# Two more weight sums moved from adding DMA transfers to VectorE, in ten units of a decoder layer

## The chip, the cores and the metric

The kernel runs on one core of a Trainium2 chip. The metric is the device time of one execution in microseconds (us), lower is better. TensorE (PE) multiplies, VectorE (DVE) and ScalarE (ACT) work elementwise, GpSimd (POOL) issues the adding DMA transfers, SyncE (SP) issues the plain loads in the order of its own queue. All five run their own instruction lists in order and meet only at semaphores.

## The reference

One layer on x of 512 positions by 2048 channels, all float32. The part that matters is a set of large products with weights:

```python
h = rmsnorm(x, norm_g[l])
proj = h @ w_in[l]                    # 2048 x 13312, three mixers and their gates
(a_u, a_b, a_c, a_z, b_v, b_g, b_z, c_u, c_z, gates) = jnp.split(proj, SPLIT_POINTS, axis=-1)
y_a = short_conv_mixer(...)           # 3-tap conv, then @ w_br_a (1024 x 2048)
y_b = conformer_conv_mixer(...)       # 31-tap conv, layernorm, then @ w_br_b
y_c = pool_mixer(...)                 # causal means, group products, then @ w_br_c
g = jax.nn.sigmoid(gates.reshape(bsz, seq, N_BRANCH, D_MODEL))
merged = g[:, :, 0] * y_a + g[:, :, 1] * y_b + g[:, :, 2] * y_c
x = x + merged @ w_o[l]               # 2048 x 2048
return rmsnorm(x, final_g)
```

## The kernel before

**Units, products, stages.** Every product with `w_in` and `w_o` is cut into units of 1024 output columns (`UNITS`: two of `glu`, four of `prod`/`side`, two of `pool`, one `zed`, six `gate`; then two for `w_o`). In a unit, positions and inner channels are halved, and a Strassen scheme makes seven products instead of eight. Each product needs one combination of the unit's four weight quarters 11, 12, 21, 22, and each combination is handled in four blocks of 128 x 1024 values (512 KB). One block of one product is a stage, so a unit has 28 stages, numbered through the program: the fourth gate unit is stages 336 to 363, the third is 308 to 335, the first unit of `w_o` is 468 to 495. Tiles carry the number: `wl350` belongs to stage 350.

**A stage.** The raw block is split into a high part (`wh`, a rounding cast by ACT, line 171) and a low part (`wl = raw - wh`, a subtraction by DVE, line 172), and TensorE makes twelve multiplications of 512 columns: lines 443 and 444 read `wh`, line 445 reads `wl`. `wh` and `wl` have three buffers each, so ACT and DVE work up to three stages ahead of TensorE.

**Where the combinations come from.** `PRODUCTS` lists the seven in order. "load" is a plain load issued by SP into a new raw tile (line 141). "add" is a transfer issued by POOL that adds a second block from memory into the raw tile already there (line 143), which can start only when the split of the block before has read that tile. "sum" is an addition by DVE of another raw tile that is loaded anyway (line 151). Raw tiles of tag A have four buffers for a unit's `11`, `s1`, `s2`, `22`; those of tag B have a ring of six for `s4`, `s3`, `12`.

```python
PRODUCTS = (
    ("11", "A", "load", 0, 0),
    ("s1", "A", "add", 0, 1),
    ("s2", "A", "sum", 1, 1),
    ("s4", "B", "load", 1, 1),
    ("s3", "B", "add", 0, 1),
    ("12", "B", "load", 1, 0),
    ("22", "A", "add", 1, 0),
)
```

**What sets the order.** `plan()` gives each transfer the stage before which it stands in the program, and a list scheduler then orders every engine's instructions; splits and sums go ahead of other DVE work where both could run. DVE work that is not about weights (31-tap convolution, line 584; centring; pooling; the activation of branch B, lines 655 to 661; joins of partial products, line 456) is handed out at a fixed rate per half stage while the units run. Its inputs (`c`, `z`, `cu`, `cz`, line 230) are loaded through the same SP queue as the raw tiles, and so are the residual rows `y` (line 1002) during `w_o`.

Of the kernel before, what the change touches and what calls it, by code (L numbers as in the profile page):

```python
# [8 lines left out]
F32 = mybir.dt.float32  # L9
# [4 lines left out]
P = 128  # L14
# [14 lines left out]
RAW = 2 * CH  # L29
# [16 lines left out]
UNITS = [("glu", B_V + c, B_G + c) for c in (0, CH)]  # L46
for _c in (0, CH):
# [10 lines left out]
# [6 lines that stand above are left out]
    ("12", "B", "load", 1, 0),  # L64
    ("22", "A", "add", 1, 0),
)
EARLY = (PRODUCTS[0], PRODUCTS[5], *PRODUCTS[1:5], PRODUCTS[6])
FIRST = (PRODUCTS[0], PRODUCTS[5], PRODUCTS[1], ("s2", "A", "add", 1, 1), *PRODUCTS[3:5], PRODUCTS[6])
STEPS = KD // 4


def block(unit, row, col, s):
    return ((unit * 2 + row) * 2 + col) * STEPS + s
# [4 lines left out]
WO_UNIT = WO_AT // (4 * STEPS)  # L78
# [8 lines left out]
def stages():  # L87

    out = []

    def seven(u, products):
        for name, tag, what, row, col in products:
            key = (u, tag, name == "12")
            out.extend((tag, key + (s,), what, block(u, row, col, s)) for s in range(STEPS))

    for u in range(len(UNITS)):
        seven(u, PRODUCTS if u else FIRST)
    for n, b in enumerate(range(BR_AT, WO_AT)):
        out.append(("AB"[n % 2], b, "load", b))
    for u in range(2):  # L100
        seven(WO_UNIT + u, EARLY if u else PRODUCTS)
    return out


class Weights:
# [3 lines left out]
    def __init__(self, tc, nc, pools, parts, src, load_ahead, split_ahead):  # L109
        self.tc, self.nc, self.pools, self.parts, self.src = tc, nc, pools, parts, src  # L110
        self.load_ahead, self.split_ahead = load_ahead, split_ahead
        self.stages = stages()
        self.last = {s[1]: n for n, s in enumerate(self.stages)}
        self.raw, self.held, self.done = {}, {}, {}
        self.events = deque(self.plan())
        self.summed = self.split = self.at = 0

    def plan(self):


        need, before, out = {}, {}, []
        for n, (_, key, what, b) in enumerate(self.stages):
            if what == "sum":
                need[b] = n - 2
            else:
                need.setdefault(b, n)
        for n, (_, key, what, b) in enumerate(self.stages):
            if what == "load":
                out.append((min(need[b], n) - self.load_ahead, n))
            elif what == "add":  # L130
                out.append((max(n - self.load_ahead, before[key] + 1), n))
            before[key] = n
        return sorted(out)

    def transfer(self):
        n = self.events.popleft()[1]
        tag, key, what, b = self.stages[n]
        if what == "load":
            t = self.raw[key] = self.held[b] = self.pools[tag].tile([P, RAW], F32, tag=tag, name=f"raw{tag}{n}")
            for at in self.pieces(n):  # L140
                self.nc.sync.dma_start(out=t[:, at], in_=self.src[b][:, at])
        else:
            self.nc.gpsimd.dma_start(out=self.raw[key], in_=self.src[b], accum_op=ALU.add)  # L143

    def sum_to(self, n):
        while self.summed < min(n, len(self.stages)):
            _, key, what, b = self.stages[self.summed]
            if what == "sum":
                t = self.raw[key]
                with self.tc.high_priority(AHEAD):  # L150
                    self.nc.vector.tensor_tensor(out=t, in0=t, in1=self.held[b], op=ALU.add)
            self.summed += 1
# [959 lines left out]
```

## Time and profile before

| quantity | value |
|---|---|
| median of 3 runs | 1652.32 us (1649.66 to 1655.26) |
| the profiled execution | 1651.81 us, of which 1650.1 us are the span |
| PE, DVE, ACT busy, share of the span | 98%, 72%, 48% |
| adding transfers of POOL (A and B) | 140 + 68, 512 KB each |
| plain raw loads of SP (A and B) | 91 + 160, 512 KB each |

The span is the time from the first to the last instruction that the profiler saw; the rest of the execution's time lies around it. Busy shares are averages over the whole span, and an engine that is busy 98% leaves little room, so what counts is where TensorE waits. A line such as `[2.67 <-DVE wl L172]` behind an instruction says that its engine sat idle for 2.67 us before it and that the end of a DVE instruction of line 172 ended that wait.

### The profile page before, as it was taken

The page shows a single profiled execution, that of the slowest core. Times are in us where ns is not written, and L with a number is a line of the kernel's source. Part 1 is how long each engine was busy: PE and PEld are TensorE (multiplying, and loading weights), DVE is VectorE, ACT ScalarE, POOL GpSimd, SP SyncE. Part 2 cuts the span into 40 slices and gives each one's busy share as a digit, 9 for nine tenths or more (in the row PEclk, how much of TensorE's full clock was granted, in tenths as well). Part 3 has the DMA queues.
Part 4 walks back from the last instruction along what each step waited for, and adds up shares of the span by engine and source line. Part 5 has one row for each costly group of instructions (what it writes and reads, how often), then busy time and mean ns, then how long its engine had stood idle before and what let it go on. Part 6 is the DMA issues. An engine that isn't in the chain of part 4 may idle for free.

```text
span 1650.1 us, 19665 instructions
## 1 busy us (share of the span) xinstructions
PE 1617.2 (98%) x7212; PEld 1330.2 (81%) x7212; DVE 1191.3 (72%) x1459; ACT 786.4 (48%) x1011; POOL 181.0 (11%) x215
## 2 busy tenths in 40 slices
PE   7899999999999999999999999999999999999997
PEld 5788887788888888888888878888888888888786
DVE  4866699899979969977778876555743444477766
ACT  6755443444444454456645454444731311345544
POOL 1201011111102020201010101010100000002010
PEclk9999999999999999999999999999999999999999
DMA  9978685968777797789989898878994633357865
GB/s 306 239 198 200 171 192 117 225 148 206 149 202 148 200 209 192 166 232 241 297 186 281 207 294 170 232 171 257 236 316 144 196 102 90 116 142 165 218 152 151
DMA packets 113744, 324.43 MB, mean 197 GB/s; under 512 B 12528, under 2 KB 16752, under 8 KB 113648
## 3 DMA queue, kind: packets, MB, share of 16 engines
q0 software_dynamic: 29952, 109.07, 36.0%
q1 hardware_dynamic: 64544, 179.50, 34.1%
q10 hardware_dynamic: 19152, 34.62, 5.7%
q8 instruction: 56, 0.92, 0.2%
q14 instruction: 40, 0.33, 0.1%
HBM read 287.48 MB, written 35.65 MB: 196 GB/s over the span
## 4 chain that ended last, share of the span: by engine, by line
PE 72%; issue 16%; DMA 6%; DVE 2%; POOL 2%; ACT 1%; SPq 0%; POOLq 0%; ACTq 0%; DVEq 0%
PE X L445 11%; PE X L443 11%; PE X L444 11%; PE Z L445 5%; PE Z L443 5%; PE Z L444 5%; PE y L897 4%; PE y L898 4%; PE y L899 4%; DMA rawB<-wts 3%; PE V L443 3%; PE V L444 3%; PE V L445 3%; POOL rawA L143 2%; DMA rawA<-wts 2%
## 5 line engine op out<-in xcount | busy, mean ns | idle before, releaser
L172 DVE TENSOR_TENSOR wl<-rawA,wh 128x1024 fp32r<-128x1024 f32 (+1 forms) x297 | 360.8, 1217 | 191.7 <-ACT wh L171 185.6
L171 ACT CAST wh<-rawA 128x1024 fp32r<-128x1024 f32 (+1 forms) x297 | 311.6, 1051 | 390.5 <-PE X L444 117.4
L172 DVE TENSOR_TENSOR wl<-rawB,wh 128x1024 fp32r<-128x1024 f32 x228 | 277.9, 1221 | 206.8 <-ACT wh L171 205.2
L171 ACT CAST wh<-rawB 128x1024 fp32r<-128x1024 f32 x228 | 238.9, 1052 | 328.6 <-PE y L898 93.2
L143 POOL DMA_DIRECT2D rawA<-wts x140 | 121.1, 865 | 1299.8 <-DVE wl L172 1262.2
L443 PE MATMUL X<-wh,xs 128*128 128x512 f32 x544 | 213.7, 393 | 3.9 <-ACT wh L171 3.8
L444 PE MATMUL X<-wh,xs 128*128 128x512 f32 x544 | 213.2, 392 | 0.0
L443 PE MATMUL Z<-wh,xs 128*128 128x512 f32 x544 | 211.4, 390 | 1.7 <-ACT xs L362 1.1
L444 PE MATMUL Z<-wh,xs 128*128 128x512 f32 x544 | 212.0, 390 | 0.7 <-DVE xs L363 0.7
L443 PE MATMUL X<-wh,x 128*128 128x512 f32 x528 | 207.2, 394 | 4.2 <-ACT x L362 4.0
L444 PE MATMUL X<-wh,x 128*128 128x512 f32 x528 | 206.8, 392 | 1.1 <-DVE x L363 1.1
L445 PE MATMUL X<-wl,xs 128*128 128x512 f32 x544 | 192.7, 393 | 7.2 <-DVE wl L172 7.0
L445 PE MATMUL Z<-wl,xs 128*128 128x512 f32 x544 | 192.5, 390 | 0.2
L445 PE MATMUL X<-wl,x 128*128 128x512 f32 x528 | 190.9, 395 | 0.0
L584 DVE SCALAR_TENSOR_TENSOR conv<-v,prm,conv 128x511 f32<-128x511 f32 (+14 forms) x240 | 168.5, 727 | 0.0
L897 PE MATMUL y<-wh,u 128*128 128x512 f32 x384 | 149.7, 390 | 0.0
L899 PE MATMUL y<-wl,u 128*128 128x512 f32 x384 | 149.7, 390 | 0.0
L898 PE MATMUL y<-wh,u 128*128 128x512 f32 x384 | 149.7, 390 | 0.0
L445 PEld LDWEIGHTS X<-wl,xs 128*128 128x128 f32 x544 | 102.1, 189 | 31.7 <-DVE wl L172 10.9
L443 PEld LDWEIGHTS X<-wh,xs 128*128 128x128 f32 x544 | 103.0, 189 | 28.1 <-ACT wh L171 6.6
L443 PEld LDWEIGHTS Z<-wh,xs 128*128 128x128 f32 x544 | 102.0, 188 | 24.2 <-ACT xs L362 1.5
L443 PEld LDWEIGHTS X<-wh,x 128*128 128x128 f32 x528 | 99.5, 189 | 26.0 <-ACT x L362 4.5
(174 smaller groups left out, 2102.6 us busy)
## 6 DMA issues: line engine op xcount, KB each, us to landing
rawB<-wts SPq DMA_DIRECT2D x160, 512.0 KB, 4.6
rawA<-wts POOLq DMA_DIRECT2D x140, 512.0 KB, 6.9
rawA<-wts SPq DMA_DIRECT2D x91, 512.0 KB, 4.2
rawB<-wts POOLq DMA_DIRECT2D x68, 512.0 KB, 8.8
g<-g SPq DMA_DIRECT2D x48, 256.0 KB, 5.0
d<-turn ACTq DMA_DIRECT2D x32, 256.0 KB, 6.4
g<-snap ACTq DMA_DIRECT2D x24, 256.0 KB, 5.4
g<-gate ACTq DMA_DIRECT2D x24, 256.0 KB, 5.7
```

The costliest lines, as they stand in the source:

```text
L143: self.nc.gpsimd.dma_start(out=self.raw[key], in_=self.src[b], accum_op=ALU.add)
L171: self.nc.scalar.copy(out=h[:, at], in_=raw[:, at])
L172: self.nc.vector.tensor_tensor(out=l[:, at], in0=raw[:, at], in1=h[:, at].bitcast(F32), op=ALU.subtract)
L443: T.matmul(p, lhsT=xh, rhs=h, start=start and k == 0, stop=False, skip_group_check=True)
L444: T.matmul(p, lhsT=xl, rhs=h, start=False, stop=False, skip_group_check=True)
L445: T.matmul(p, lhsT=xh, rhs=l, start=False, stop=k == KB - 1, skip_group_check=True)
L584: V.scalar_tensor_tensor(out=c[:, s:], in0=v[:, : S - s], scalar=pcol(P_BW, i * CONV_B + CONV_B - 1 - s), in1=c[:, s:], op0=ALU.mult, op1= ...
L897: T.matmul(banks[t], lhsT=uh[:, tk], rhs=h, start=k == 0, stop=False)
L898: T.matmul(banks[t], lhsT=ul[:, tk], rhs=h, start=False, stop=False)
L899: T.matmul(banks[t], lhsT=uh[:, tk], rhs=l, start=False, stop=k == KB - 1)
```

## The change

In the units of `pool`, `zed` and `gate` and in the first unit of `w_o` (ten units), two of the three "add" products become DVE sums (`ROOM`). For `s3` a new kind, "both", loads its block into a raw tile of its own and DVE then adds the raw tile of `s4` to it. For `22`, DVE adds the raw tile of `12`, which is loaded anyway, so no transfer is left. The last unit of `w_o` gets only the `s3` part (`EARLY`). `s1` stays an adding transfer.

```diff
+ROOM = (*PRODUCTS[:4], ("s3", "B", "both", 0, 1), PRODUCTS[5], ("22", "A", "sum", 1, 0))
+EARLY = (PRODUCTS[0], PRODUCTS[5], *PRODUCTS[1:4], ROOM[4], PRODUCTS[6])
...
-        seven(u, PRODUCTS if u else FIRST)
+        seven(u, ROOM if UNITS[u][0] in ("pool", "zed", "gate") else PRODUCTS if u else FIRST)
...
-        seven(WO_UNIT + u, EARLY if u else PRODUCTS)
+        seven(WO_UNIT + u, EARLY if u else ROOM)
...
             if what == "sum":
-                need[b] = n - 2
+                need[b] = min(need.get(b, n), n - 2)
...
+            elif what == "both":
+                out.append((n - 2 - self.load_ahead, n))
...
-        if what == "load":
-            t = self.raw[key] = self.held[b] = self.pools[tag].tile([P, RAW], F32, tag=tag, name=f"raw{tag}{n}")
+        if what in ("load", "both"):
+            t = self.raw[key] = self.pools[tag].tile([P, RAW], F32, tag=tag, name=f"raw{tag}{n}")
...
+            if what == "load":
+                self.held[b] = t
...
-            if what == "sum":
+            if what in ("sum", "both"):
                 t = self.raw[key]
+                if what == "both":
+                    b += 2 * STEPS
                 with self.tc.high_priority(AHEAD):
                     self.nc.vector.tensor_tensor(out=t, in0=t, in1=self.held[b], op=ALU.add)
```

Over the program POOL loses 84 adding transfers (44 of `s3`, 40 of `22`), SP gains 44 plain loads, and DVE gains 84 sums. In the changed kernel the sum stands on line 160, the split's subtraction on line 181, the plain load on line 146, the join on line 465, the fill on line 239 and the residual load on line 1011.

DVE in the fourth gate unit, before, from the split of the first `s4` block on (`rawB348` to `rawB351` are its four raw tiles; `s3` is added into the same tiles, so stages 352 and 353 read `rawB348` and `rawB349` again):

```order
L172 TENSOR_TENSOR wl348_8067<-rawB348_7874,wh348_8066 128x1024
L172 TENSOR_TENSOR wl349_8084<-rawB349_7893,wh349_8083 128x1024
L172 TENSOR_TENSOR wl350_8105<-rawB350_7912,wh350_8104 128x1024
L172 TENSOR_TENSOR wl351_8122<-rawB351_7938,wh351_8121 128x1024
L172 TENSOR_TENSOR wl352_8141<-rawB348_7874,wh352_8140 128x1024
L172 TENSOR_TENSOR wl353_8159<-rawB349_7893,wh353_8158 128x1024
L456 TENSOR_TENSOR snap_584_8099<-Z_580_7960,snap_584_8099 128x512
L456 TENSOR_TENSOR snap_585_8100<-Z_581_7961,snap_585_8100 128x512
L172 TENSOR_TENSOR wl354_8185<-rawB350_7912,wh354_8184 128x1024
```

The same place in the changed kernel, from behind `wl349` on (`rawB352` to `rawB355` are the new tiles of `s3`, `rawB356` to `rawB359` those of `12`, and `rawA336` to `rawA339` become the blocks of `22`):

```order
L160 TENSOR_TENSOR rawB354_8118<-rawB354_8118,rawB350_7960 128x1024
L181 TENSOR_TENSOR wl350_8159<-rawB350_7960,wh350_8158 128x1024
L160 TENSOR_TENSOR rawB355_8136<-rawB355_8136,rawB351_7986 128x1024
L181 TENSOR_TENSOR wl351_8176<-rawB351_7986,wh351_8175 128x1024
L160 TENSOR_TENSOR rawA336_7766<-rawA336_7766,rawB356_8192 128x1024
L181 TENSOR_TENSOR wl352_8195<-rawB352_8082,wh352_8194 128x1024
L160 TENSOR_TENSOR rawA337_7797<-rawA337_7797,rawB357_8211 128x1024
L181 TENSOR_TENSOR wl353_8214<-rawB353_8100,wh353_8213 128x1024
L465 TENSOR_TENSOR snap_584_8154<-Z_580_8008,snap_584_8154 128x512
L160 TENSOR_TENSOR rawA338_7826<-rawA338_7826,rawB358_8238 128x1024
L465 TENSOR_TENSOR snap_585_8155<-Z_581_8009,snap_585_8155 128x512
L181 TENSOR_TENSOR wl354_8241<-rawB354_8118,wh354_8240 128x1024
```

Five sums now stand between the splits of stages 349 and 354, each ahead of the split of the next stage. The first two sums of `s3` (`rawB352`, `rawB353`) stand earlier, at the end of the unit before. With six buffers in the ring, `rawB354` takes the buffer of `rawB348`, `rawB356` that of `rawB350`, `rawB358` that of `rawB352`, and the odd numbers likewise.

SP's queue in the third gate unit, before, near the end of the activation of branch B (`c` and `z` are its inputs; `rawB330` and `rawB331` are the last two blocks of `12`; all other raw loads of the unit stand further ahead):

```order
L230 DMA c_540_7538<-cd_388_6106 128x512
L230 DMA z_541_7540<-d_350_5809 128x512
L230 DMA c_546_7612<-cd_390_6135 128x512
L230 DMA z_547_7614<-d_353_5831 128x512
L230 DMA c_550_7664<-cd_392_6160 128x512
L230 DMA z_551_7666<-d_356_5840 128x512
L141 DMA rawB330_7582<-wts 128x1024
L230 DMA c_558_7732<-cd_396_6204 128x512
L141 DMA rawB331_7600<-wts 128x1024
```

The same place in the changed kernel:

```order
L146 DMA rawB326_7454<-wts 128x1024
L239 DMA c_534_7522<-cd_384_6098 128x512
L239 DMA z_535_7524<-d_347_5824 128x512
L146 DMA rawB327_7482<-wts 128x1024
L239 DMA c_540_7584<-cd_388_6136 128x512
L239 DMA z_541_7586<-d_350_5833 128x512
L146 DMA rawB328_7572<-wts 128x1024
L239 DMA c_546_7660<-cd_390_6165 128x512
L239 DMA z_547_7662<-d_353_5855 128x512
L146 DMA rawB329_7603<-wts 128x1024
L146 DMA rawB330_7630<-wts 128x1024
L239 DMA c_550_7710<-cd_392_6190 128x512
```

The six raw loads that wait for a buffer of the ring (`rawB326` to `rawB331`) now stand between the loads of `c` and `z`.

SP's queue in the first unit of `w_o`, before, behind the residual loads (`rawB490` and `rawB491` are the last two blocks of `12`; `rawB500` belongs to the last unit):

```order
L1002 DMA y_882_11746<-xn 128x512
L1002 DMA y_883_11747<-xn 128x512
L141 DMA rawB490_11858<-wts 128x1024
L141 DMA rawB491_11876<-wts 128x1024
L141 DMA rawB500_12066<-wts 128x1024
```

The same place in the changed kernel:

```order
L1011 DMA y_882_11824<-xn 128x512
L1011 DMA y_883_11825<-xn 128x512
L146 DMA rawB486_11802<-wts 128x1024
L146 DMA rawB487_11828<-wts 128x1024
L146 DMA rawB488_11884<-wts 128x1024
L146 DMA rawB489_11903<-wts 128x1024
L146 DMA rawB490_11938<-wts 128x1024
L146 DMA rawB491_11956<-wts 128x1024
L146 DMA rawB500_12146<-wts 128x1024
```

Two blocks of `s3` and all four of `12` now stand behind the eight residual loads; before, `s3` had no load, and two blocks of `12` stood there.

## Rows read from the trace of the kernel before

**Rows 1.** The page: busy time by engine, share of the span, instructions.

```profile
PE 1617.2 (98%) x7212; PEld 1330.2 (81%) x7212; DVE 1191.3 (72%) x1459; ACT 786.4 (48%) x1011; POOL 181.0 (11%) x215
```

**Rows 2.** Busy time by stretch: first pool unit, zed, third gate.

```profile
core 0: us, PE busy (x) PEld busy (x) DVE busy (x) ACT busy (x) POOL busy (x), PEclk, DMA share, GB/s
490.00:568.00 78.00, 77.94 (x352) 64.26 (x352) 76.27 (x95) 34.40 (x39) 10.36 (x12) 1.00 0.74 170
...
648.00:730.00 82.00, 81.66 (x375) 67.28 (x374) 71.90 (x85) 42.58 (x53) 10.38 (x12) 1.00 0.79 194
...
896.00:978.00 82.00, 79.33 (x343) 65.19 (x342) 63.20 (x86) 41.16 (x50) 10.41 (x12) 0.98 0.94 254
```

**Rows 3.** Timeline of PE around four gaps: zed, first gate, third gate, `w_o`.

```profile
701.54 0.50 PE L443 MATMUL X<-wh,xs 128*128 128x512 f32 x1 [0.28 <-ACT wh L171]
...
781.80 0.39 PE L444 MATMUL Z<-wh,xs 128*128 128x512 f32 x1
782.91 0.50 PE L443 MATMUL X<-wh,xs 128*128 128x512 f32 x1 [0.73 <-ACT wh L171]
...
951.96 0.39 PE L444 MATMUL X<-wh,xs 128*128 128x512 f32 x1
955.02 0.73 PE L445 MATMUL X<-wl,xs 128*128 128x512 f32 x2 [2.67 <-DVE wl L172]
...
1526.09 0.39 PE L445 MATMUL Z<-wl,xs 128*128 128x512 f32 x1
1527.83 0.50 PE L443 MATMUL X<-wh,xs 128*128 128x512 f32 x1 [1.35 <-ACT wh L171]
```

**Rows 4.** Timeline of ACT: the casts just ahead of the second and fourth gap.

```profile
781.81 1.04 ACT L171 CAST wh<-rawB 128x1024 fp32r<-128x1024 f32 x1 [4.27 <-DMA rawB<-wts]
...
1526.73 1.04 ACT L171 CAST wh<-rawB 128x1024 fp32r<-128x1024 f32 x1 [7.55 <-DMA rawB<-wts]
```

**Rows 5.** Timeline of DVE at the third gap; then the stretch behind it, columns as in Rows 2.

```profile
952.53 0.69 DVE L655 TENSOR_TENSOR c<-c,rstd 128x512 f32<-128x512 f32 x1 [3.75 <-DMA c<-cd]
953.14 0.69 DVE L660 TENSOR_TENSOR c<-c,z 128x512 f32<-128x512 f32 x1
953.75 1.22 DVE L172 TENSOR_TENSOR wl<-rawB,wh 128x1024 fp32r<-128x1024 f32 x1
954.88 0.68 DVE L456 TENSOR_TENSOR snap<-Z,snap 128x512 f32<-128x512 f32 x1
...
955.80:959.00 3.20, 3.20 (x9) 2.49 (x8) 3.20 (x6) 2.85 (x5) 0.00 (x0) 0.50 0.88 220
```

**Rows 6.** The page: DMA queues; then DMA issues (count, size, median us to landing).

```profile
q0 software_dynamic: 29952, 109.07, 36.0%
q1 hardware_dynamic: 64544, 179.50, 34.1%
...
rawB<-wts SPq DMA_DIRECT2D x160, 512.0 KB, 4.6
...
rawB<-wts POOLq DMA_DIRECT2D x68, 512.0 KB, 8.8
```

**Rows 7.** Timeline of the fourth gate unit: DVE splits, a use by PE, SP's loads.

```profile
1014.05 1.22 DVE L172 TENSOR_TENSOR wl<-rawB,wh 128x1024 fp32r<-128x1024 f32 x1 [1.49 <-ACT wh L171]
1016.78 1.22 DVE L172 TENSOR_TENSOR wl<-rawB,wh 128x1024 fp32r<-128x1024 f32 x1 [1.50 <-ACT wh L171]
...
1019.34 0.62 PE L445 MATMUL Z<-wl,xs 128*128 128x512 f32 x2
...
1024.93 1.23 DVE L172 TENSOR_TENSOR wl<-rawB,wh 128x1024 fp32r<-128x1024 f32 x1 [1.49 <-ACT wh L171]
...
1026.19 19.37 SPq L141 DMA_DIRECT2D rawB<-wts  x8
```

**Rows 8.** Plain raw loads by SP (line 141), 484 to 568 us.

```profile
DMA to landing us min/median/max: 3.5/4.0/6.3
```

**Rows 9.** The same, 1008 to 1210 us.

```profile
DMA to landing us min/median/max: 3.5/4.5/5.8
```

More of the change, by code (lines that the diff above doesn't have):

```diff
@@ L66 @@
 )
-EARLY = (PRODUCTS[0], PRODUCTS[5], *PRODUCTS[1:5], PRODUCTS[6])
+ROOM = (*PRODUCTS[:4], ("s3", "B", "both", 0, 1), PRODUCTS[5], ("22", "A", "sum", 1, 0))
+EARLY = (PRODUCTS[0], PRODUCTS[5], *PRODUCTS[1:4], ROOM[4], PRODUCTS[6])
 FIRST = (PRODUCTS[0], PRODUCTS[5], PRODUCTS[1], ("s2", "A", "add", 1, 1), *PRODUCTS[3:5], PRODUCTS[6])
@@ L92, in seven @@
         for name, tag, what, row, col in products:
-            key = (u, tag, name == "12")
+            key = (u, tag, name == "12", what == "both")
             out.extend((tag, key + (s,), what, block(u, row, col, s)) for s in range(STEPS))
     for u in range(len(UNITS)):
-        seven(u, PRODUCTS if u else FIRST)
+        seven(u, ROOM if UNITS[u][0] in ("pool", "zed", "gate") else PRODUCTS if u else FIRST)
     for n, b in enumerate(range(BR_AT, WO_AT)):
```

## Prediction

> **What bounds the kernel now.** The page's busy times come first: PE is busy 98% of the span, DVE 72%, POOL 11% [rows 1]. So only the places where PE waits can give time back, and whatever makes PE wait costs time. The stretches show how even that is: in the first pool unit PE is busy 77.94 of 78.00 us, in zed 81.66 of 82.00, in the third gate unit 79.33 of 82.00 [rows 2]. The timeline of PE then shows the gaps in the ten units that the change touches. Four carry nearly all: 0.28 us idle in zed; 1.11 us from start to start in the first gate unit, where 0.23 is normal; 3.06 us in the third gate unit; 1.74 us in the first unit of `w_o` [rows 3].
>
> What released them says whether the change can help. The casts ahead of the second and fourth gap waited 4.27 and 7.55 us for the transfer into `rawB` [rows 4], and at this place, the step from Z (`s4`) to X (`s3`), that is the adding transfer of `s3`: it starts only when the split of `s4` has read the tile, and lands after a median of 8.8 us, against 4.6 for a plain load into rawB [rows 6]. The third gap is indirect: DVE's split stood behind an instruction that waited 3.75 us for `c` from memory [rows 5], in a stretch whose DMA engines are 94% busy [rows 2].
>
> **What is removed.** Zed 0.3. First gate unit 1.11 - 0.23 = 0.9. Third gate unit 3.06 - 0.23 = 2.8, and behind it the granted clock is 0.50, so the 1.2 GHz level, for 3.2 us [rows 5]: half of that, 1.6, is lost as well, 4.4 in all. `w_o` 1.74 - 0.23 = 1.5. Sum: 0.3 + 0.9 + 4.4 + 1.5 = 7.1 us, 0.4%; beyond this nothing that the change touches keeps PE waiting for long, so it is about the most that it can give.
>
> Will all of it go? An adding transfer takes 36.0% of 1650 us over 208 transfers = 2.9 us of all DMA engines, a plain 512 KB takes 34.1% of 1650 over 179.5/0.524 = 343 blocks = 1.6 us [rows 6]. A unit loses eight adds and gains four loads, 23 - 6.5 = 16 us of DMA time, which takes the third gate unit from 94% to about 74%. With that, `c` should land in time, although raw loads that wait for a buffer now stand between the loads of `c` and `z` in SP's queue. I take back all but 1 us there.
>
> **What is added to DVE.** A sum has the shape of the split's subtraction, 1.13 us from start to start (953.75 to 954.88), so eight cost 9.1 us a unit. Where DVE has room, that hides behind PE. In the first pool unit it has none: 76.27 of 78.00 busy [rows 2], the new order there puts seven convolution taps fewer (0.61 us each by the nearest row, 952.53 to 953.14) and one other instruction more, 76.3 + 9.1 - 4.3 + 0.6 = 81.7 us of work in 78. Zed: 71.9 + 9.1 + six taps 3.7 - three others 1.8 = 82.9 in 82.0. The cover is DVE's lead: the split that starts at 1014.05 ends at 1015.27 and is first read at 1019.34, so DVE may be 4.07 us late before PE waits [rows 7]. The overhang of 3.7 us in the pool unit just fits under it, and the next unit has room. I take 1 us each for these two, since the lead is not full at all times; without the cover it would be 4.6 us together.
>
> **The new wait.** `s3` gets a tile of its own, so twelve tiles a unit pass through a ring of six, and in the new order a chain runs through it: split of stage 348 frees a buffer, load of `rawB354`, sum, split 350, load of `rawB356`, sum, split 352, load of `rawB358`, sum, split 354. DVE is in order, so a sum that waits for its load holds the next split, and PE stands behind that. Each link is 1.26 us from the start of the split to the load's issue (1024.93 to 1026.19), the landing L, and 1.13 for the sum; one join of 0.6 stands in the last. From split 348 to split 354 that is 3L + 7.8, and PE's pace needs 6 x 2.73 = 16.4 (1014.05 to 1016.78) [rows 7]. The lateness is 3L - 8.6, and beyond the lead of 4.07 PE stops: at L = 4.2 us. The medians of plain raw loads are 4.0 in one stretch and 4.5 in another, minimum 3.5, maximum 6.3 [rows 8, 9]. So this hangs on tenths: L = 4.0 gives nothing, 4.5 gives 3 x 4.5 - 12.7 = 0.8 us a unit, 5.0 gives 2.3. The ends are nothing (3.5) and 6.2 us a unit (6.3 in every load); since three landings add up, the medians are the nearest rows. They lie around 4.25, and part of the adding transfers that shared the engines is gone; I take 4.3: 0.2 us in each of seven units, 1.4 us (the first pool unit and zed are counted above).
>
> The Trainium skill, DMA: Bandwidth & Descriptors, section Anatomy of one DMA, fits a transfer as about 2.0 us plus its bytes over 436 GB/s; for 512 KB that is an estimate of 3.2 us, and the chain would be 1 us late at the end, under the lead. The trace doesn't bear it out for this mix: the fastest plain load took 3.5 us [rows 8, 9], and the fit is for a transfer by itself.
>
> **`w_o`.** Two loads of `s3` and four of `12` now stand behind eight residual loads, and the chain runs there too. I take back half of what is removed: 0.8 us of 1.5 stays. The `s3` part in the last unit meets no gap of its own; 0.
>
> **Sum.** -7.1 removed, +1 (third gate unit), +2 (DVE work), +1.4 (ring), +0.8 (`w_o`) = -1.9; against the profiled 1651.8 us that is 1649.9. The median of the runs is 0.5 above the profiled execution: 1650.4 us. No change would be within 0.3%, 5 us, which is about what a measurement of this kernel can tell.
>
> **Rivals.**
>
> *The ring never binds* and DVE's lead covers the sums: L stays at 3.5 to 4.0 with the adds gone. Then 6 to 7.1 us are gained: 1645.2 to 1646.3. For it: the minimum of 3.5, and 16 us less DMA work a unit. The fit of the Trainium skill, an estimate of 3.2 us for a block, would end here. Against it: 4.5 us is the median even from 1008 to 1210, where fewer adds overlap with the loads. Chance 0.27.
>
> *The ring binds in every unit*, the one on the other side. The place is the sum of `rawB358` ahead of split 354, the price 3L - 12.7 us in nine units. With 1 + 2 + 0.8 - 7.1 = -3.3 for the rest, the change is slower by 5 us from 9(3L - 12.7) = 8.3 on, so from L = 4.55; at 5.0 it is 1652.3 + 17.4 = 1669.7. A stop of 3 us also brought the low clock [rows 3, 5]. For it: the 6.3 and 5.8 at the top, and loads in the DVE-heavy units that share SP's queue. Against it: the lead starts full in each unit, since the eight stages behind the chain have no such wait. Chance 0.22.
>
> *The waits only move*: the third gate unit keeps its gap, since `c` and `z` now queue behind raw loads that wait for the ring, and the saved waits on adds equal the new ones. Sum -7.1 + 4.4 + 2 + 1.4 + 0.8 = +1.5, 1653.8. Chance 0.15.
>
> **Chances and range.** My forecast has 0.36 and spans 1647 to 1652.5. Faster by over 0.3% (under 1647.3) is the first rival and a little of mine: 0.31. Slower (over 1657.3) is the second rival: 0.23 with a little of the third. Same: 0.46. The range goes from 1644 (all is gained and nothing new binds, with 1 us for the spread of the runs) to 1662 (L = 4.75 in all nine units: 9 x 1.55 - 3.3 = 10 above 1652.3), which leaves out somewhat under 0.2.
>
> **What would show it.** Right: POOL's adds fall from 208 to 124; the casts of `s3` no longer wait for `rawB`; no gap at Z to X in zed and the first gate unit; the DMA share of the third gate unit falls to about 0.75 and its 3 us gap goes; the new sums wait for `rawB` landings, with idle time ahead of line 160; PE stops are small and lie at stages 354 and 355 of a unit's kind (`s3`, third and fourth block). Wrong: gaps of over 1 us there in most units, landings of 5 us or more in the chain, a longer first pool unit, or `c` landing late as before.

## The result, and the profile after

The changed kernel takes 1661.63 us, the median of 9 runs (1657.50 to 1668.13), and the kernel before takes 1654.78 us in 9 runs beside it. The ratio is 1.0051, with a 95% interval of 1.0037 to 1.0065, so the change costs 8.4 us (6 to 11). A second series of 10 runs gave 1.0047 (1.0030 to 1.0065). The prediction was 1650.4 us. The measured median lies at the far end of the range, and on the other side of no change.

The page of the changed kernel first: busy times, the DMA queues, the group of the sums, and the plain and adding loads (count, size, median us to landing). They answer to [rows 1, 6].

```profile
PE 1622.3 (98%) x7212; PEld 1331.6 (80%) x7212; DVE 1278.7 (77%) x1543; ACT 787.8 (47%) x1011; POOL 108.7 (7%) x131
...
q0 software_dynamic: 17856, 65.02, 21.1%
...
rawB<-wts SPq DMA_DIRECT2D x204, 512.0 KB, 4.1
rawA<-wts POOLq DMA_DIRECT2D x100, 512.0 KB, 7.4
...
rawB<-wts POOLq DMA_DIRECT2D x24, 512.0 KB, 9.0
```

The moved work is as foreseen: 124 adding transfers in place of 208, 44 more plain loads, DVE busy 87 us more. The adding queue's share of the DMA engines fell from 36.0% to 21.1%, and the plain loads of ring B land in 4.1 us in place of 4.6. But PE is busy 5 us longer for the same 7212 multiplications: the ends of pipelined multiplications are modelled, so part of a small stop counts as busy. At 822.65 below, for one, the page gives 0.45 us idle, and the step from start to start is 0.61 us too long.

The stretches show where DVE stands: first pool unit, second pool unit, zed, third gate unit.

```profile
497.00:578.00 81.00, 80.38 (x360) 65.48 (x359) 81.00 (x96) 34.93 (x38) 3.47 (x4) 1.00 0.52 143
578.00:661.00 83.00, 80.92 (x371) 66.32 (x370) 75.13 (x87) 41.43 (x50) 3.46 (x4) 1.00 0.60 167
661.00:742.00 81.00, 80.93 (x373) 66.71 (x371) 80.57 (x96) 41.95 (x51) 3.46 (x4) 1.00 0.57 160
911.00:992.00 81.00, 80.48 (x352) 65.31 (x351) 72.66 (x96) 41.83 (x51) 3.25 (x4) 1.00 0.77 242
```

In the third gate unit the DMA share is as predicted, 0.77 where it was 0.94 [rows 2], and the clock is 1.00. In the first pool unit DVE has no time left at all, 81.00 of 81.00 us, and in zed next to none, 80.57 of 81.00.

**Where PE stands still.** A unit's length misleads, because the order moves some multiplications from one unit to its neighbour. So the stops are counted: each step from the start of one multiplication to the next that is longer than 0.33 us gives what exceeds the usual 0.227 us; steps at the low clock count too. The table adds these up by unit, from the first pool unit on, from the timeline of PE, one profile a line (us):

```
                        pool1 pool2  zed  gate1 gate3  w_o 1  w_o 2
before                   0.3   0.3   0.6   1.0   4.5    2.7    2.2
before, second profile   0.3   0.3   0.0   0.6   2.7    2.4    2.3
before, third profile    0.3   0.3   0.0   1.7   2.3    2.0    2.5
changed                  1.9   2.5   1.5   2.1   1.5    0.0    7.7
changed, second profile  2.0   2.5   1.2   2.1   1.5    0.0    7.8
```

The gate units that are not shown have none. Added up it is 11.6, 8.6 and 9.1 us before, 9.8 in the mean, and 17.2 and 17.1 after: 7.4 us more, which is nearly all of the 8.4 and 7.8 measured. The code ahead of the first pool unit is the same in both kernels; its stops are not, and "What is chance?" below takes them up. The losses sit in three places: the two pool units, zed, and above all the last unit of `w_o`, where the prediction had put 0.

**The pool units.** DVE's timeline in the second pool unit, at the last blocks of `s3` and at those of `22` (the rows between 630.53 and 644.29 are left out), and the wait of PE that follows:

```profile
619.08 1.22 DVE L181 TENSOR_TENSOR wl<-rawB,wh 128x1024 fp32r<-128x1024 f32 x1 [1.49 <-ACT wh L180]
621.29 1.23 DVE L160 TENSOR_TENSOR rawB<-rawB,rawB 128x1024 f32<-128x1024 f32 x1 [0.99 <-DMA rawB<-wts]
622.43 1.00 DVE L586 TENSOR_SCALAR conv<-v,prm 128x512 f32<-128x512 f32 x2
623.35 1.22 DVE L181 TENSOR_TENSOR wl<-rawB,wh 128x1024 fp32r<-128x1024 f32 x1
624.48 1.41 DVE L593 SCALAR_TENSOR_TENSOR conv<-v,prm,conv 128x511 f32<-128x511 f32 x2
625.80 1.22 DVE L160 TENSOR_TENSOR rawB<-rawB,rawB 128x1024 f32<-128x1024 f32 x1
626.94 1.22 DVE L181 TENSOR_TENSOR wl<-rawB,wh 128x1024 fp32r<-128x1024 f32 x1
628.07 1.41 DVE L593 SCALAR_TENSOR_TENSOR conv<-v,prm,conv 128x510 f32<-128x510 f32 x2
629.39 1.22 DVE L160 TENSOR_TENSOR rawA<-rawA,rawB 128x1024 f32<-128x1024 f32 x1
630.53 1.22 DVE L181 TENSOR_TENSOR wl<-rawB,wh 128x1024 fp32r<-128x1024 f32 x1
...
644.29 1.22 DVE L181 TENSOR_TENSOR wl<-rawB,wh 128x1024 fp32r<-128x1024 f32 x1
...
645.56 0.73 PE L454 MATMUL V<-wl,x 128*128 128x512 f32 x2 [1.62 <-DVE wl L181]
```

The first of the sums waits 0.99 us for its block, whose load was issued at 617.61, when the split at 616.36 had just freed a tile of the ring; this wait is there, 0.8 to 1.3 us long, in all seven profiles that have both sums in this unit on DVE, and the taps. Behind it DVE is never idle: it waits for nothing and is still late. From split to split (623.35, 626.94, 630.53) a stage takes 3.59 us: a split, a sum, two taps. PE needs 2.73 for a stage [rows 7]. Six sums follow each other, two of `s3` and four of `22`, and joins and activations of other work come between. The seven stages from 619.08 to 644.29 take 25.2 us where PE's pace needs 19.1, so DVE falls 6.1 us behind, 1.0 of it by the wait for the block. The lead of 4.07 us is used up; at 645.56 PE waits 1.62 us for a split. In the first pool unit no sum waits for a block, and PE stops all the same.

**The last unit.** DVE's timeline, then SP's queue in the same place, and PE's first wait:

```profile
1586.58 1.23 DVE L181 TENSOR_TENSOR wl<-rawA,wh 128x1024 fp32r<-128x1024 f32 x1 [1.49 <-ACT wh L180]
1590.77 1.22 DVE L160 TENSOR_TENSOR rawB<-rawB,rawB 128x1024 f32<-128x1024 f32 x1 [2.96 <-DMA rawB<-wts]
1591.91 1.22 DVE L160 TENSOR_TENSOR rawA<-rawA,rawB 128x1024 f32<-128x1024 f32 x1
1593.05 1.22 DVE L160 TENSOR_TENSOR rawB<-rawB,rawB 128x1024 f32<-128x1024 f32 x1
1594.19 1.22 DVE L181 TENSOR_TENSOR wl<-rawA,wh 128x1024 fp32r<-128x1024 f32 x1
...
1580.28 1.87 SPq L1011 DMA_DIRECT2D y<-xn  x2
1583.55 1.90 SPq L146 DMA_DIRECT2D rawB<-wts  x2
...
1595.46 0.50 PE L454 MATMUL Z<-wl,xs 128*128 128x512 f32 x1 [1.16 <-DVE wl L181]
```

The sum of the first `s3` block stands ahead of a split in DVE's order. Its load is issued at 1583.55, behind eight residual loads, and lands 7.1 us later, when DVE has waited 2.96 us. Two more sums follow before the split, which starts 7.6 us after the one before it in place of 2.7.

**The ring**, on which the prediction spent most words, makes DVE wait, and PE seldom. Sums wait for their blocks as the prediction foresaw; the first line is the trace's account for line 160 over the whole program (us in total, times). Plain raw loads (line 146) landed as follows from 497 to 742 us, from 742 to 992 us (the first three gate units), from 992 to 1221 us (the last three), and from 1569 us on (the last unit):

```profile
  DMA rawB<-wts: 31.8, 26
...
DMA to landing us min/median/max: 3.4/3.7/6.3
...
DMA to landing us min/median/max: 3.6/4.6/7.5
...
DMA to landing us min/median/max: 3.4/3.9/6.3
...
DMA to landing us min/median/max: 4.5/7.0/8.4
```

The medians of 3.7 and 3.9 us are under the 4.2 us from which PE was to stop, and in the last three gate units it does not stop, although sums there wait up to 3.4 us. The median of 4.6 us is above it, and there two waits reach PE, at the end of the first gate unit and at that of the third, each at the first of the two sums of `s3` that stand there:

```profile
820.23 1.23 DVE L160 TENSOR_TENSOR rawB<-rawB,rawB 128x1024 f32<-128x1024 f32 x1 [2.79 <-DMA rawB<-wts]
...
822.65 0.73 PE L454 MATMUL X<-wl,x 128*128 128x512 f32 x2 [0.45 <-DVE wl L181]
826.45 0.73 PE L454 MATMUL X<-wl,x 128*128 128x512 f32 x2 [0.79 <-DVE wl L181]
...
985.45 1.23 DVE L160 TENSOR_TENSOR rawB<-rawB,rawB 128x1024 f32<-128x1024 f32 x1 [1.85 <-DMA rawB<-wts]
...
991.33 0.73 PE L454 MATMUL X<-wl,x 128*128 128x512 f32 x2 [0.47 <-DVE wl L181]
```

### The profile page after: what moved, and what is told of

It is laid out like the page before. It is cut to its first block, busy times and chain, and to the rows that moved or that the text cites. A ratio compares the mean times of both kernels' runs of the same rounds, so it can differ in the third digit from the quotient of the medians.

```text
span 1662.9 us, 19592 instructions
## 1 busy us (share of the span) xinstructions
PE 1622.3 (98%) x7212; PEld 1331.6 (80%) x7212; DVE 1278.7 (77%) x1543; ACT 787.8 (47%) x1011; POOL 108.7 (7%) x131
## 3 DMA queue, kind: packets, MB, share of 16 engines
q0 software_dynamic: 17856, 65.02, 21.1%
## 4 chain that ended last, share of the span: by engine, by line
PE 42%; DVE 5%; issue 4%; DMA 2%; POOL 0%; ACT 0%; POOLq 0%; DVEq 0%; SPq 0%
PE y L906 5%; PE y L907 5%; PE y L908 5%; PE X L454 5%; PE X L453 5%; PE X L452 5%; PE Z L454 2%; PE Z L453 2%; PE Z L452 2%; DVE wl L181 2%; DMA rawB<-wts 1%; PE V L453 1%; PE V L454 1%; PE V L452 1%; DMA rawA<-wts 1%
## 5 line engine op out<-in xcount | busy, mean ns | idle before, releaser
L150 POOL DMA_DIRECT2D rawA<-wts x100 | 86.8, 868 | 1455.9 <-DVE wl L181 1110.4
L160 DVE TENSOR_TENSOR rawA<-rawA,rawB 128x1024 f32<-128x1024 f32 x104 | 126.7, 1219 | 7.2 <-DMA rawB<-wts 6.5
L454 PEld LDWEIGHTS Z<-wl,xs 128*128 128x128 f32 x544 | 102.9, 190 | 29.8 <-DVE wl L181 8.4
L452 PEld LDWEIGHTS Z<-wh,xs 128*128 128x128 f32 x544 | 103.0, 190 | 26.3 <-ACT wh L180 3.2
```

What stands on the lines that cost most here:

```text
L452: T.matmul(p, lhsT=xh, rhs=h, start=start and k == 0, stop=False, skip_group_check=True)
L454: T.matmul(p, lhsT=xh, rhs=l, start=False, stop=k == KB - 1, skip_group_check=True)
```

## The experiments

Each kernel was run beside the kernel before; the ratio is to that, with its 95% interval. "Stops" are those of the table above. In the expectations of the first four runs, theory A stands for DVE's order (sums beside the splits in the pool units, sums ahead of the splits in the last unit), and its rival for the ring of six tiles and the loads that it delays.

**Parts of the change.** First the last unit alone goes back: its `s3` is added on the way in again.

```diff
-EARLY = (PRODUCTS[0], PRODUCTS[5], *PRODUCTS[1:4], ROOM[4], PRODUCTS[6])
+EARLY = (PRODUCTS[0], PRODUCTS[5], *PRODUCTS[1:5], PRODUCTS[6])
```

> The changed kernel with the last unit's s3 put back to an adding transfer; the rest of the change stays. Theory A (two places lose: the last unit, where a sum waits behind residual loads, and the two pool units, where DVE has no room left): the last unit falls back from 93.7 to about 88 us, so the kernel is some 5 us faster than the changed one and 2 to 3 us slower than before: ratio 1.0015 to 1.002. Theory B (the ring of six raw tiles holds splits up in every unit, the last one is only a part of run-to-run spread): no more than 1 to 2 us come back, ratio 1.004 or more.

Measured: 1656.71 us, 1.0022 (1.0007 to 1.0038). The stops of the last unit are 2.2 us, as before, in place of 7.7. So 5.5 us belong to `s3` in the last unit. The rest of the change still does not gain.

Then only `22` by DVE, or only `s3`, both with the last unit as before.

```diff
+ROOM = (*PRODUCTS[:6], ("22", "A", "sum", 1, 0))
```

> Only 22 becomes a DVE sum in the ten units; s3 stays an adding transfer everywhere, so the ring carries eight tiles a unit as before and DVE gets four sums a unit, not eight. Theory A: the pool units lose half or less (DVE 4 x 1.14 = 4.6 us a unit), the last unit nothing, the third gate unit and the first unit of w_o gain: 1 to 4 us faster than before, ratio 0.9975 to 0.9995. Theory B: without the ring's chain all new waits go: 4 to 7 us faster, ratio 0.996 to 0.9975.

```diff
+ROOM = (*PRODUCTS[:4], ("s3", "B", "both", 0, 1), *PRODUCTS[5:])
```

> Only s3 becomes a load into a tile of its own with a DVE sum, in the ten units; 22 stays an adding transfer, the last unit is as before. Four sums a unit, twelve tiles a unit in the ring. Theory A: like the kernel with only 22, since DVE gets the same four sums: within 2 us of it. Theory B: the ring's chain stays, so it is slower than the kernel with only 22 by 4 us or more, and slower than before.

Measured: 1657.63, 1.0039 (1.0025 to 1.0053), and 1657.41, 1.0032 (1.0021 to 1.0043). The two are level, as theory A had it, but both are slower than before, which neither reading had foreseen for `22` alone. With `22` alone the adds of `s3` stay, and so do their stops: zed 2.1, third gate 3.9, first `w_o` unit 3.8 us, and the first pool unit has 2.0. With `s3` alone zed has 1.5 and the other two 0.0, but the pool units have 2.0 and 3.1, and the second and fourth gate units 2.6 and 1.4, where no other kernel stops. So it takes `s3` to clear the stop in `w_o`, and `s3` is also what costs in the second pool unit.

Next both sums where DVE has room: the six gate units and the first `w_o` unit (the last unit as before).

```diff
-        seven(u, ROOM if UNITS[u][0] in ("pool", "zed", "gate") else PRODUCTS if u else FIRST)
+        seven(u, ROOM if UNITS[u][0] in ("gate",) else PRODUCTS if u else FIRST)
```

> Both new sums in the six gate units and the first unit of w_o only; pool, zed and the last unit as before. Theory A: the DVE-full units are spared, what is left is the gain of the first and third gate unit and of w_o: 4 to 8 us faster than before, ratio 0.995 to 0.9975. Theory B: six units with the ring's chain still lose what they gain: ratio 0.999 to 1.002.

Measured: 1649.03, 0.9981 (0.9971 to 0.9992), faster than both kernels, by less than expected. Stops: pool units 0.3 each, zed 0.0, first gate 1.3, third gate 1.0, `w_o` 0.0.

**Is it DVE's work or the ring, in the pool units?** The two kernels that follow leave out 30 of the 31 taps of the convolution, and with them that work of DVE: one is the kernel before, the other the changed one with the last unit as before.

```diff
-        return [(0.5, first)] + [(0.7, lambda s=s: tap(s)) for s in range(1, CONV_B)] + [(0.7, last)]
+        return [(0.5, first)] + [(0.7, lambda: None) for s in range(1, CONV_B)] + [(0.7, last)]
```

> The kernel before without 30 of the convolution taps of branch B (left out of the computation), so that VectorE has less to do in the two pooling units. By the theory that VectorE was no limit there before: the two pooling units take 78.4 and 79.4 us as before (within 0.7 us each), and the ratio is 0.999 to 1.001.

> The change with the last unit's s3 left as an addition on the way in, and without the same 30 taps (left out of the computation). VectorE theory (sums, splits and taps that stand side by side use up the lead in the pooling units): the units fall from 81.3 and 82.8 us to 78.4 and 79.4 (within 0.7 us each), and the time falls about 5 us below that of the same kernel with taps, to a ratio of 0.997 to 0.999. Ring theory (the fifth and sixth loads wait for a free tile, and what waits for them is late): the taps change nothing, the pooling units stay at 81 and 82.5 us, ratio 1.002.

Measured: 1649.60, 0.9988 (0.9969 to 1.0006), without the taps in the kernel before, and 1643.26, 0.9945 (0.9927 to 0.9963), with the change. The two pool units of the second, 78 and 80 us:

```profile
490.00:568.00 78.00, 78.00 (x353) 64.49 (x352) 57.80 (x57) 36.10 (x40) 3.46 (x4) 1.00 0.53 148
568.00:648.00 80.00, 80.00 (x370) 66.54 (x370) 56.36 (x55) 41.27 (x50) 3.45 (x4) 1.00 0.60 172
```

With DVE busy 58 and 56 us, PE is busy throughout. The stops in the pool units and in zed are 0.0 in both kernels, although the same sums still wait for loads in the same ring (6.9 us in nine waits, in the pool units of the second). So the waits for loads alone don't stop PE there: it is DVE's work that uses up the lead. In zed the last link is a load all the same: with the taps, the split of the first block of `22` ends at 735.91, the load of the next unit's first block into its tile is issued at 735.94 and takes 6.3 us, and PE stops at 743.48 for the cast of that block. The time fell by 13.4 us against the same kernel with the taps, where some 5 were expected; the stops from the first pool unit on account for 6.6. The taps run from 195 us on, so the units ahead lose that work of DVE too; what this gives there was not measured by itself. With no taps in either kernel the change gains 6.3 us (1649.60 to 1643.26).

The same from the other side: a seventh tile in the ring, in the whole change.

```diff
-    rb = ctx.enter_context(tc.tile_pool(name="rb", bufs=6))
+    rb = ctx.enter_context(tc.tile_pool(name="rb", bufs=7))
-    tp = ctx.enter_context(tc.tile_pool(name="tp", bufs=20))
+    tp = ctx.enter_context(tc.tile_pool(name="tp", bufs=18))
```

> The whole change with seven raw tiles in ring B in place of six (two of the 512-column scratch tiles are given up for it). Ring theory: the loads of s3 are issued a stage earlier everywhere, so the pooling units fall from 81.0 and 82.4 us towards 78.4 and 79.4, and the last unit from 93.7 to 88 to 90; ratio 0.998 to 1.001. VectorE theory (it is the work that stands side by side that uses up the lead): the pooling units stay at 81 and 82.5 us within 0.7; ratio 1.002 to 1.005.

Measured: 1664.75, 1.0079 (1.0060 to 1.0097). The pool units have 2.4 and 3.2 us of stops, no less than with six tiles, where the ring theory had them fall. The run does not take the wait for a block away, though: the order puts the sums a tile further ahead, and in the second pool unit one waits 1.06 us again, so the ring's 1.0 us there stays untested. Nor is it shown what the two scratch tiles fewer cost. The last unit became worse, 9.9 us: the order now puts the first sum ahead of one more split, and DVE waited 5.73 us for its load.

The pool units alone, all else as before:

```diff
+        seven(u, ROOM if UNITS[u][0] in ("pool",) else PRODUCTS if u else FIRST)
...
+        seven(WO_UNIT + u, EARLY if u else PRODUCTS)
```

> Both sums in the two pooling units alone, all else as before. VectorE theory: the units take 81.1 and 82.4 us in place of 78.4 and 79.4, 5.7 us more, ratio 1.0035 if nothing is given back behind them. If the loss came from the whole of the change (its loads in the other units), they take 78.5 to 79.5 and the ratio is 1.000.

Measured: 1655.75, 1.0015 (0.9999 to 1.0032). The stops are 1.9 and 2.3 us, as in the whole change: the loss there is the pool units' own. Zed has 0.0 then; its 1.1 us (the means are given further down) come when its own sums follow on those of the pool units.

Last, the eight sums of each pool unit by GpSimd, with the last unit as before:

```diff
-                    self.nc.vector.tensor_tensor(out=t, in0=t, in1=self.held[b], op=ALU.add)
+                    (self.nc.gpsimd if key[0] < len(UNITS) and UNITS[key[0]][0] == 'pool' and (what == 'both' or self.summed % 28 >= 24) else self.nc.vector).tensor_tensor(out=t, in0=t, in1=self.held[b], op=ALU.add)
```

> The change with the last unit's s3 left as an addition on the way in, and in the two pooling units the eight new sums of each (s3's four and 22's four) made by GpSimd in place of VectorE: the same loads, tiles and order. VectorE theory: the pooling units fall from 81.3 and 82.8 us to 78 to 79.8, ratio 0.997 to 0.999, if GpSimd's sum of 128x1024 takes under about 3 us (no trace of this case shows one). Ring or load theory: they stay at 81 and 82.5 us or more, ratio 1.002.

Measured: 1678.34, 1.0155 (1.0131 to 1.0179), with stops of 15.2 and 10.7 us. It doesn't tell the theories apart: its condition was a sum of under about 3 us, and GpSimd's sixteen took 2.35 to 3.60, at a price for DVE that the last section shows.

**What in the last unit costs 5.4 us?** First the residual loads go to ACT's queue.

```diff
-            nc.sync.dma_start(out=ys[t, cg], in_=xn[t, :, cg * CH : (cg + 1) * CH])
+            (nc.scalar if u else nc.sync).dma_start(out=ys[t, cg], in_=xn[t, :, cg * CH : (cg + 1) * CH])
```

> The whole change, with the residual loads of the last unit issued by ScalarE in place of SyncE. Queue theory (the first s3 load of the last unit stands behind eight of these loads on SyncE's queue, lands at 1590.68, and VectorE's sum of it holds up the split behind it): that load lands 4 us or more earlier, and the last unit falls from 93.7 us to 88 to 89.5; ratio 1.002. Order theory (that VectorE adds three s3 blocks ahead of the splits costs the time by itself): the unit stays at 92 to 94 us, ratio 1.005.

Measured: 1660.34, 1.0047 (1.0030 to 1.0063); stops 7.3 us, no better. DVE's row of the place, the sum behind the split:

```profile
1588.36 1.23 DVE L160 TENSOR_TENSOR rawB<-rawB,rawB 128x1024 f32<-128x1024 f32 x1 [3.04 <-DMA rawB<-wts]
```

DVE still waits 3.04 us. The queue alone is not it, but the run did not take the lateness away either: the wait of SP only moved, to a residual load's landing. The waits of SP's queue there for such a landing (us in total, times, longest):

```profile
SPq L146 <- DMA y<-xn: 6.4, 2, 5.3
```

So the residual loads were left out.

```diff
-            nc.sync.dma_start(out=ys[t, cg], in_=xn[t, :, cg * CH : (cg + 1) * CH])
+            nc.gpsimd.memset(ys[t, cg], 0.0) if u else nc.sync.dma_start(out=ys[t, cg], in_=xn[t, :, cg * CH : (cg + 1) * CH])
```

> The whole change, in which the last unit's residual rows are not loaded but set to zero by GpSimd (the residual of the second half of the columns is left out of the computation), so that its eight loads are gone from the queues. Late-load theory (the first s3 load of the last unit is held up by the residual loads, on SyncE's queue as in the changed kernel, or by their landing as in the run with them on ScalarE, where the load was issued at 1582.87 after a wait for one of them): VectorE no longer waits about 3 us for it, and the last unit falls from 93.7 us to 88.5 to 91. Order theory (three sums ahead of a split cost the time by themselves): it stays at 92 to 94.

Measured: 1656.79, 1.0027 (1.0013 to 1.0040); stops 6.7 us. DVE's rows at the place, and two stretches at the later `s3` blocks (columns as in Rows 2):

```profile
1579.30 1.23 DVE L160 TENSOR_TENSOR rawB<-rawB,rawB 128x1024 f32<-128x1024 f32 x1 [1.81 <-DMA rawB<-wts]
1580.44 1.22 DVE L181 TENSOR_TENSOR wl<-rawA,wh 128x1024 fp32r<-128x1024 f32 x1
1581.76 1.23 DVE L160 TENSOR_TENSOR rawB<-rawB,rawB 128x1024 f32<-128x1024 f32 x1
1582.90 1.22 DVE L160 TENSOR_TENSOR rawA<-rawA,rawB 128x1024 f32<-128x1024 f32 x1
1584.04 1.22 DVE L181 TENSOR_TENSOR wl<-rawA,wh 128x1024 fp32r<-128x1024 f32 x1
...
1612.00:1616.00 4.00, 2.24 (x9) 1.25 (x8) 3.85 (x4) 3.93 (x6) 0.00 (x0) 0.99 0.39 127
1616.00:1620.00 4.00, 4.00 (x12) 3.09 (x12) 3.06 (x3) 1.04 (x1) 0.00 (x0) 0.59 0.00 0
```

The four raw loads of the place land in 4.1 to 4.6 us here, against 6.8 to 8.4 in the changed kernel: what made the load late is for the most part its slow landing beside the residual loads, not its place in the queue. The wait that is left fell into a gap that DVE had anyway. By the start of each stage's first multiplication, the unit is 2.0 us behind the kernel before after sixteen stages, against 4.7 in the changed kernel: 2.6 us were the late load. The other 2.0 stay with loads in time: sums, splits and output work follow on DVE without a break, as in the pool units. At the later blocks both kernels stop again where the last two sums stand between splits. In the run without residual loads the granted clock is 0.59 in the 4 us behind that stop, most of them at the 1.2 GHz level, where the changed kernel stayed at 1.00; these slow steps are 1.6 of its 6.7 us, and without them it would be 5.1, again 2.6 under the 7.7. So neither theory is the whole: about half of the 5.4 us is the late load, the other half the sums themselves.

**The best version.** Both sums in zed, the gate units and the first `w_o` unit (pool and last unit as before):

```diff
+        seven(u, ROOM if UNITS[u][0] in ("zed", "gate") else PRODUCTS if u else FIRST)
```

> Both sums in zed, the six gate units and the first w_o unit; pooling and last unit as before. By the sums per unit (zed -2, first gate unit +0.5 to +1.5 against the version with the gates alone): zed and the first gate unit together 161.0 to 162.8 us, ratio 0.997 to 0.9985, the same as or up to 1.5 us faster than the gates alone.

Measured: 1649.02, 0.9979 (0.9966 to 0.9993): faster than both kernels, and level with the gates alone. Zed's stops are 0.3 us with its sums, so what zed loses in the whole change comes only with the pool units' sums ahead of its own.

**What is chance?** A profile is one execution, so the kernel before was profiled twice more, the changed one once more, and a kernel was run that changes the first `w_o` unit alone:

```diff
+        seven(u, PRODUCTS if u else FIRST)
...
+        seven(WO_UNIT + u, EARLY if u else ROOM)
```

> The kernel before once more, unchanged, for a second profile. In the one profile of it the first two units took 92.4 + 78.9 = 171.3 us on TensorE, in those of the changed kernel and of four variants 174.2 to 180.8 us, although the instructions of these units are the same in all. If that is chance, the two units come out anywhere from 171 to 181 us here, and the ratio is 1.000 within 0.001. If something that follows in the changed kernel slows them, they take 171 to 172.5 us again.

> The kernel before a third time. If the wait for v in the first 460 us is chance, it may show here too; if it belongs to programs with the change, the third unit takes 78.7 to 79 us again.

> The changed kernel once more, unchanged, for a second profile. In four profiles of it and of its variants that differ only in the last unit, the first 460 us, whose instructions are those of the kernel before, held a wait of VectorE for v from memory (4.5 us in the first one) that neither profile of the kernel before held; only one of the four was without it. If that is chance, this profile may go either way, and the ratio is 1.005. The changed units repeat: pooling 81 and 82.4 us, zed 80.3, last unit 93.7.

> Both sums in the first w_o unit alone; the first 1,480 us are those of the kernel before. By the time per unit: 78.0 in place of 80.9 us, ratio 0.998. If programs with the change lose about 3 us in stretches that they leave as they were, the ratio is 1.000.

Measured: 1.0001 (0.9987 to 1.0015), 0.9999 (0.9983 to 1.0015), 1.0047 (1.0030 to 1.0065), and 0.9984 (0.9968 to 1.0001), 2.8 us less, for the `w_o` unit alone, as its stops (2.4 to 0.0) say. The wait of DVE for `v` in the first 460 us showed in the third profile of before with 0.33 us, in the changed kernel's two with 4.46 and 3.10. PE, DVE and ACT have the same instructions in the same order up to 483 us in fifteen of the profiles. Eleven of these are of kernels that change pool, zed or gate units: eight have the wait with 2.7 us or more, three with 0.4 or less. The other four, whose units up to `w_o` are those of before, have none above 0.33. All stops ahead of the first pool unit, which the table leaves out, add up to 25.6 to 26.3 us in these four, to 32.7 and 30.8 in the changed kernel's two, and to 26.7 to 33.8 in the other nine. So it is not shown that this is chance: the four lie below all the others, and no cause was found. The measured times show how much it can be: the change costs 0.4 to 1.0 us more than the stops of the table, and the pool units alone 2.5 us where their stops (12.5 us against 9.8) say 2.7. The three profiled executions of before took 1651.8, 1650.1 and 1649.9 us, under the medians of its runs in every series (1652.3 to 1654.8), so part of the difference between the profiles is not in the medians. The kernel with the last unit as before measured 3.6 us over the kernel before (1.2 to 6.3), where its stops add up to 10.0; that is open.

## Why the prediction was wrong

Means over the three profiles of before, and over five of code that is the same up to the last unit (the changed kernel twice, and those with the last unit back, with residuals on ACT and without residuals); for the last unit, over the changed kernel's two.

- **"What is added to DVE", the step that failed first.** The prediction took 1 us each for the first pool unit and zed, and nothing for the second pool unit ("the next unit has room"). Measured: 1.7, 1.1 and 2.2 us, so 5.0 in place of 2. The unit's total was nearly right, 81.7 us of work in the first pool unit where DVE is now busy 81.00 of 81.00. What failed was to hold an average overhang against the lead. The second unit has room as a whole (75.13 of 83.00), and yet it loses most: eight sums do not spread over it, six stand side by side in stages that carry taps as well. The seven stages from 619.08 on take 3.60 us each against 2.73, 6.1 us in all, and the lead is 4.07; what is left, 2.0 us, is PE's stop at 645.56. About 1.0 of it is the first sum's wait for its block, a wait of the kind that the step on the ring had; the rest is DVE's work. The order of the changed kernel's rows shows the sums side by side; the prediction did not price them there.
- **"The `s3` part in the last unit meets no gap of its own; 0", the largest miss.** Measured: +5.4 us. The sentence looked for a gap to remove and found none; it did not ask what the new sum brings. The order has it ahead of a split and ahead of two sums, and its load behind the residual loads that the step on `w_o` had counted for the first unit only; beside them it took 7.1 us to land.
- **"Removed": the mechanism was right, one size was not.** Casts of `s3` no longer wait for an adding transfer. The first `w_o` unit gives all of its 2.4 us; the prediction kept half of 1.5. The third gate unit gives 2.1 in place of 3.4 net (4.4 less the 1 kept): the gap of 3.06 us with the low clock behind it [rows 3, 5] is not in every execution. In the second profile of before (and alike in the third) `c` was late too, and PE had two shorter stops with the clock at 1.00. The kernel that changes the first `w_o` unit alone, whose code is that of before up to there, had one stop of 1.88 us idle, with the low clock behind it and 3.7 us in all. The rows show the second profile of before, then PE's stop in that kernel and the stretch behind it (columns as in Rows 2):

```profile
951.02 0.69 DVE L655 TENSOR_TENSOR c<-c,rstd 128x512 f32<-128x512 f32 x1 [3.08 <-DMA c<-cd]
...
953.51 0.74 PE L445 MATMUL X<-wl,xs 128*128 128x512 f32 x2 [1.19 <-DVE wl L172]
957.50 0.73 PE L445 MATMUL X<-wl,xs 128*128 128x512 f32 x2 [0.98 <-DVE wl L172]
...
953.67 0.73 PE L454 MATMUL X<-wl,xs 128*128 128x512 f32 x2 [1.88 <-DVE wl L181]
...
955.00:958.00 3.00, 3.00 (x9) 2.31 (x8) 3.00 (x5) 2.68 (x4) 0.00 (x0) 0.55 0.95 319
```

  The first gate unit and zed were to give 1.2 together. The old gaps are gone; the first gate unit's mean is 1.3 us of stops against 1.1, since the sum's wait at 820.23 took their place.
- **"The new wait": 1.4 us predicted**, 0.2 in each of seven units. Measured: 1.3 us in the first gate unit, which takes the place of the old 1.1 there, part of the 1.1 us that the third gate unit keeps, and about 1.0 of the second pool unit's; nothing in the others. The form of the term held: by its own formula the median of 4.6 us in the first three gate units gives 1.1 us each, and the medians of 3.7 and 3.9 elsewhere give nothing. One L for all units, 4.3, was the weak point, and so was the place: the waits that reach PE in the gate units stand at the first block of `s3`, at the end of the unit before, not at the third and fourth. The Trainium skill, DMA: Bandwidth & Descriptors, section Anatomy of one DMA, has a fit for transfers issued by GpSimd that would give an estimate of 3.2 us for such a block; SP's loads in the changed kernel took 3.4 us at the least in the four stretches above.
- **The sum.** Pool units and zed +5.0, first gate +0.2, third gate -2.1, first `w_o` unit -2.4, last unit +5.4: +6.1 us, against -1.9 predicted and 7.8 to 8.4 measured, with intervals from 5.0 to 10.8. About 2 us are in none of these terms. The table's 7.4 us, from the changed kernel's own two profiles, comes closer; the runs don't show whether what is left lies ahead of the first pool unit.
- **The rivals.** The first of them, that the ring never binds, was right for PE in most units, though not for DVE, whose sums waited 26 times; had DVE's term been right, the result would have lain nearer to it. The second had the right sign by the wrong mechanism: its chance of slower stood on the ring alone. None of the rivals had DVE's pile-up, which the term of 2 us should have made one.

## What to carry to other kernels

Where an in-order engine feeds the one that sets the pace, sum its work over the stretch in which the new instructions stand, stage by stage, and hold that against its lead; an average over the unit hides a pile-up that a neighbour's slack can't pay for. Ask of each new instruction what stands behind it and when its input lands, also where no gap of before is at stake. And size a gap from several executions: the stops of the third gate unit were 2.3 to 4.5 us in four executions of the same code.

## What was not expected of the hardware

**GpSimd and VectorE hold each other up.** With the pool units' sums on GpSimd, its rows and DVE's beside them are:

```profile
555.18 3.05 POOL L160 TENSOR_TENSOR rawA<-rawA,rawB 128x1024 f32<-128x1024 f32 x1 [1.49 <-DMA rawB<-wts]
559.51 3.28 POOL L160 TENSOR_TENSOR rawA<-rawA,rawB 128x1024 f32<-128x1024 f32 x1 [1.28 <-DMA rawB<-wts]
...
555.93 3.48 DVE L593 SCALAR_TENSOR_TENSOR conv<-v,prm,conv 128x493 f32<-128x493 f32 x2
560.46 3.51 DVE L593 SCALAR_TENSOR_TENSOR conv<-v,prm,conv 128x492 f32<-128x492 f32 x2
```

The two sums take GpSimd 3.05 and 3.28 us where DVE takes 1.22, and two taps take 3.48 and 3.51 us while it runs, in place of 1.41 (624.48 above). So each of these two sums that were taken from DVE cost it 2.1 us, more than the sum itself. The Trainium skill, SBUF — State Buffer, section Who interferes with whom, says that a DVE instruction with two inputs in SBUF contends with a GpSimd instruction that reads SBUF, and that issue order decides who blocks. These rows agree: the two taps that start at 555.93 are done only after GpSimd's sum, which started at 555.18, has ended at 558.23.

**Waits for one load differ by microseconds in code that is the same.** In the third unit the first tap waits for `v` from memory. The wait was 0.33 us in the third profile of before and 4.46 in the first of the changed kernel, with the same instructions up to there; "What is chance?" above says why chance is not shown to be the cause:

```profile
200.74 0.55 DVE L586 TENSOR_SCALAR conv<-v,prm 128x512 f32<-128x512 f32 x1 [4.46 <-DMA v<-d]
```
